# Placing the matmul operands, opening stages with two output tiles at once, and re-queuing the mixers' products in a four-part transformer kernel

## The chip, the cores and the metric

The kernel runs on one core of one Trainium2 chip. The metric is the device time of one execution in microseconds (us). Engines: PE (TensorE) multiplies matrices, DVE (VectorE) and ACT (ScalarE) work element by element, POOL (GpSimd) does some additions, and SP issues most of the DMAs.

## The reference

One block with four mixers over 512 tokens of 1024 features, and then two hybrid layers. All dense products are fp32. Cut to what matters:

```python
def first_block(x, p, ...):
    z = rms_norm(x, norm1_g) @ w_in
    mix = concat([gmlp(z), rglru(z), hgrn2(z), pool(z)])
    x = x + mix @ w_out
    hf = causal_dwconv(rms_norm(x, norm2_g) @ w_up)
    x = x + (gelu(gate half) * value half) @ w_down
    x = x + (p @ w_pe) * sigmoid(rms_norm(x, norm3_g) @ w_pg)
    return rms_norm(x, final_g)

def hybrid_layer(x, ...):                       # twice
    proj = (_rms(x) * norm1_g) @ w_in           # attention, rwkv, retention, gates
    mixed = g[0] * (attention(...) @ w_attn_o) \
          + g[1] * (rwkv7_time_mix(...) @ w_rwkv_o) \
          + g[2] * (retention(...) @ w_ret_o)   # g = sigmoid(gates)
    x = x + mixed @ w_out
    h2 = _rms(x) * norm2_g
    return x + (silu(h2 @ w_ffn_gate) * (h2 @ w_ffn_up)) @ w_ffn_down
```

## The kernel before, in words

Activations lie with features on the 128 partitions and the 512 tokens along the free axis, so a 1024-feature array is eight tiles `x0` to `x7`. Each fp32 operand is written as a sum of two numbers in a shorter format (`hi` and `lo`), and a product is three matmuls: hi by hi (L135), hi by lo (L136), lo by hi (L137), in `mac`. A dense output tile over 1024 features is thus 24 matmuls of 128x128 weights and 128x512 moving data; the down products run over 22 hidden tiles, 66 matmuls.

Weights arrive from DRAM in chunks of 128x1024 (`fetch`, L114, three buffers `wraw`). `chunk` splits each into `whi` (a cast on ACT, L125) and `wlo` (a subtraction on DVE, L126), with two buffers each. Accumulators are four PSUM banks `mm` and four `ps`. The moving operands are the split tiles `x#h/x#l` (pool `xgp`), the hidden tiles `h#h/h#l` (pools `f1h`, `f2h`), the attention and retention outputs `o` (pool `op`), the mixed tiles `mx#h/mx#l` (pool `mp`) and the rwkv outputs, which reuse the `BK` tiles (pool `rk`).

The place of a tile in a partition follows from the sizes of the pools opened ahead of it. In bytes, counted from a multiple of 256: the weight buffers and all `x` tiles begin at 32; `h`, `o` and `mx` at 160; `BK` at 64.

The order of work on an engine is set by a planner at compile time: it goes through the instructions by their place in the program, takes the earliest that by its own estimate of durations is ready, and passes over those that are not; each engine then runs its list in that order and waits where an operand is not there yet. `high_priority(offset=300)` moves a weight chunk's load and conversion 300 places forward. On top of this the program itself holds a queue of fill tasks (`queue`, `pump`, `flush`): in each hybrid layer 24 gate tiles (`gate_tile`) and 16 projections of the attention and retention stage, put out a few microseconds' worth at a time between the steps of the rwkv, attention and retention mixers, each task with a stated cost.

The norm of a stage is applied after its product: `acc_sq` (L219 ACT square, L220 addition on POOL) sums the squares of eight tiles, `norm_scale` sums over features with small matmuls (L210), takes a reciprocal root in a dozen small DVE steps and broadcasts it (L195) as `rb`, by which the first outputs of the stage are scaled. In the program `norm_scale` stands ahead of the stage's first product. Stages that begin so: `ffn1` (w_up), its gate product (w_pg), each layer's projections (`rwkv`, from the scales at the end of `ffn1` or `ffn2`), `ffn2`.

In a layer, `rwkv` comes first (with `rwkv_inverse`, which keeps DVE busy with small steps and eight long transposes, L952 and L956), then `out_b` (w_rwkv_o), `branches` (attention projections, `attention`, `retention`, `combine`, w_out) and `ffn2`. `retention` works through four chunks of 128 tokens; in each, the normalised output `ot` (`head_rms`, L662 to L671) is transposed on PE (L1366), multiplied by the gate (L1370) and split (L1371, L1372). `combine` (L1378 on) then runs both remaining output products, w_attn_o and w_ret_o, and adds gates and the stored rwkv part.

Of the kernel before, what the change touches and what calls it, by code (L numbers as in the profile page):

```python
# [10 lines left out]
F32 = mybir.dt.float32  # L11
# [9 lines left out]
P = 128  # L21
# [13 lines left out]
class Kern:  # L35
# [38 lines left out]

    def tap(self, name, ap):
        if name in self.taps:
            self.nc.sync.dma_start(self.taps[name], ap)
# [33 lines left out]
    def fetch(self, src):  # L111
        raw = self.tile(self.wp, [P, 1024], "wraw", bufs=3)
# [4 lines left out]
    def chunk(self, src):  # L117
# [4 lines left out]
        hi = self.tile(self.wp, [P, 1024], "whi", F32R)  # L122
        lo = self.tile(self.wp, [P, 1024], "wlo", F32R)
# [15 lines left out]
    def dense(self, wname, m, xs, kcuts=None):  # L139
# [9 lines left out]
        return ps  # L149

# [62 lines left out]
    def acc_sq(self, acc, x, i, eng=None):  # L213
# [45 lines left out]
    def mixers1(self, c2, x, xg, rb, pe):  # L259
# [4 lines left out]
        self.tb = c2.enter_context(tc.tile_pool(name="b1tt", bufs=12))  # L264
# [408 lines left out]
    def ffn1(self, x, acc, xg, pe, xs_p):  # L673
        tc, nc, io, V = self.tc, self.nc, self.io, self.vec
        rb = self.norm_scale(acc)
        with tc.tile_pool(name="f1h", bufs=1) as hp, tc.tile_pool(name="f1t", bufs=2) as fp:
            hid = []
            for j in range(FT):
                r = []
                for half in range(2):  # L680
                    m = half * FT + j
                    ps = self.dense("w_up", 2 * j + half, xg)
# [13 lines left out]
            for m in range(DT):  # L696
# [3 lines left out]
                self.acc_sq(acc, x[m], m)  # L700
        rb = self.norm_scale(acc)

        a3 = self.tile(self.xp, [P, T], "acc", bufs=2)
        a4 = self.tile(xs_p, [P, T], "acc4")
        xd = self.tile(self.dr, [DT, P, T], "xres", bufs=4)
        with tc.tile_pool(name="f1g", bufs=2) as gp:
            for m in range(DT):
                ps = self.dense("w_pg", m, xg)
# [12 lines left out]


# [10 lines left out]
            r4b = self.tile(gp, [P, T], "r4b", bufs=1)  # L733
# [3 lines left out]
        return xd, out, rb  # L737


    def layer(self, l, xd, xg, rb, out=None):  # L740
        tc, nc, io = self.tc, self.nc, self.io
        self.l, self.xgs, self.rb = l, xg, rb
        self.gates = self.tile(self.dr, [24, P, T], "gates", bufs=2)
        self.mixb = self.tile(self.dr, [DT, P, T], "mixb", bufs=2)
        with ExitStack() as c:
            self.rwkv(c)
# [18 lines left out]
    def rwkv(self, c):  # L765
        tc, nc, io, V, l = self.tc, self.nc, self.io, self.V2, self.l
        kp = c.enter_context(tc.tile_pool(name="rk", bufs=1))
        for g in range(24):
            g = (g + 8) % 24
            self.queue(5.2, lambda g=g: self.gate_tile(g))  # L770
        self.tb = c.enter_context(tc.tile_pool(name="rt", bufs=12))
# [25 lines left out]
        AR = self.tile(kp, [P, 4, NCH, P], "AR")  # L797
        BK = [self.tile(kp, [P, NCH, P], f"BK{p}") for p in range(4)]
# [5 lines left out]
        def shifted(m, mu):  # L804
            ps = self.proj(m)
# [8 lines left out]
        wd_t = shifted(18, 12)  # L814
# [3 lines left out]
        gd_t = shifted(19, 13)  # L818
# [294 lines left out]

    def evac(self, dst, ps, scale=1.0):
# [7 lines left out]
    def branches(self, c, xd):  # L1122
        tc, nc, io, l = self.tc, self.nc, self.io, self.l
        op = c.enter_context(tc.tile_pool(name="op", bufs=1))
        with ExitStack() as c2:
            ap = c2.enter_context(tc.tile_pool(name="ap", bufs=1))
            rp = c2.enter_context(tc.tile_pool(name="rp", bufs=1))
            at = c2.enter_context(tc.tile_pool(name="at", bufs=4))
# [448 lines left out]
```

## Time and profile before

| | |
|---|---|
| median of three runs | 2609.47 us (2606.51 to 2609.70) |
| the profiled execution | 2611.01 us |
| its span, first to last instruction | 2609.2 us |
| PE busy | 2533.5 us, 97% |
| DVE, ACT, POOL busy | 1468.6, 912.1, 378.1 us |
| mean granted clock of PE | 0.992 |

The span is the time between the first and the last instruction of the profiled execution. A matmul's end is modelled in this profile, and consecutive matmuls overlap in it, so the pace of a stream of matmuls is read from the distances of their starts and not from their durations.

### The profile page before, as it was taken

The page shows a single profiled execution, that of the slowest core. Times are in us where ns is not written, and L with a number is a line of the kernel's source. Part 1 is how long each engine was busy: PE and PEld are TensorE (multiplying, and loading weights), DVE is VectorE, ACT ScalarE, POOL GpSimd, SP SyncE. Part 2 cuts the span into 40 slices and gives each one's busy share as a digit, 9 for nine tenths or more (in the row PEclk, how much of TensorE's full clock was granted, in tenths as well). Part 3 has the DMA queues.
Part 4 walks back from the last instruction along what each step waited for, and adds up shares of the span by engine and source line. Part 5 has one row for each costly group of instructions (what it writes and reads, how often), then busy time and mean ns, then how long its engine had stood idle before and what let it go on. Part 6 is the DMA issues. An engine that isn't in the chain of part 4 may idle for free. (4 is left out here: it accounts for less than half of the span.)

```text
span 2609.2 us, 33284 instructions
## 1 busy us (share of the span) xinstructions
PE 2533.5 (97%) x13104; PEld 2019.5 (77%) x13104; DVE 1468.6 (56%) x2512; ACT 912.1 (35%) x1370; POOL 378.1 (14%) x277
## 2 busy tenths in 40 slices
PE   8989999999999999999999999999999999999999
PEld 6777888887777777677788887777777677788887
DVE  8776666326787556565544433787556565444422
ACT  4343444325433334423322222433334423322211
POOL 2122111003110001005311101110001004211100
PEclk9999999999999999999999999999999999999999
DMA  4132332334224153235433234224153226332242
GB/s 151 60 110 85 96 97 96 95 98 145 93 77 134 56 180 97 73 100 192 129 97 97 95 122 132 82 82 134 58 178 93 73 95 201 128 97 97 95 121 91
DMA packets 99501, 282.51 MB, mean 108 GB/s; under 512 B 13200, under 2 KB 14224, under 8 KB 99216
## 3 DMA queue, kind: packets, MB, share of 16 engines
q1 hardware_dynamic: 97616, 277.52, 33.1%
q10 hardware_dynamic: 1728, 2.87, 0.3%
q8 instruction: 103, 1.69, 0.3%
q14 instruction: 54, 0.44, 0.1%
HBM read 244.42 MB, written 31.72 MB: 106 GB/s over the span
## 5 line engine op out<-in xcount | busy, mean ns | idle before, releaser
L125 ACT CAST whi<-wraw 128x1024 fp32r<-128x1024 f32 (+1 forms) x400 | 414.2, 1036 | 1101.4 <-PE mm L136 704.7
L126 DVE TENSOR_TENSOR wlo<-wraw,whi 128x1024 fp32r<-128x1024 f32 (+1 forms) x400 | 494.7, 1237 | 243.8 <-ACT whi L125 231.8
L1410 POOL TENSOR_TENSOR fg<-fg,rb 128x512 f32<-128x512 f32 x44 | 78.3, 1779 | 396.1 <-ACT fg L1409 396.1
L220 POOL TENSOR_TENSOR acc<-acc,sq 128x512 f32<-128x512 f32 x49 | 78.4, 1601 | 325.8 <-ACT sq L219 325.8
L135 PE MATMUL mm<-x0h,whi 128*128 128x512 f32 x286 | 117.7, 412 | 8.1 <-ACT x0h L165 8.1
L137 PE MATMUL mm<-x0h,wlo 128*128 128x512 f32 x286 | 115.1, 403 | 5.5 <-DVE wlo L126 5.4
L136 PE MATMUL mm<-x0l,whi 128*128 128x512 f32 x286 | 113.3, 396 | 1.3 <-DVE x0l L169 1.3
L136 PE MATMUL mm<-x5l,whi 128*128 128x512 f32 x286 | 112.9, 395 | 1.6 <-DVE x5l L169 1.6
L136 PE MATMUL mm<-x1l,whi 128*128 128x512 f32 x286 | 113.8, 398 | 0.3 <-DVE x1l L169 0.3
L1412 DVE TENSOR_TENSOR fg<-fg,mm 128x512 f32<-128x512 f32 x44 | 30.3, 688 | 148.9 <-PE mm L137 148.9
L136 PE MATMUL mm<-x2l,whi 128*128 128x512 f32 x286 | 113.9, 398 | 0.0
L135 PE MATMUL mm<-x1h,whi 128*128 128x512 f32 x286 | 113.8, 398 | 0.0
L135 PE MATMUL mm<-x7h,whi 128*128 128x512 f32 x286 | 113.6, 397 | 0.0
L136 PE MATMUL mm<-x3l,whi 128*128 128x512 f32 x286 | 112.8, 394 | 0.7 <-DVE x3l L169 0.7
L137 PE MATMUL mm<-x1h,wlo 128*128 128x512 f32 x286 | 113.4, 396 | 0.0
L137 PE MATMUL mm<-x2h,wlo 128*128 128x512 f32 x286 | 113.3, 396 | 0.0
L135 PE MATMUL mm<-x3h,whi 128*128 128x512 f32 x286 | 112.9, 395 | 0.0
L135 PE MATMUL mm<-x2h,whi 128*128 128x512 f32 x286 | 112.8, 394 | 0.0
L137 PE MATMUL mm<-x6h,wlo 128*128 128x512 f32 x286 | 112.8, 394 | 0.0
L136 PE MATMUL mm<-x7l,whi 128*128 128x512 f32 x286 | 112.7, 394 | 0.0
L137 PE MATMUL mm<-x5h,wlo 128*128 128x512 f32 x286 | 112.7, 394 | 0.0
L136 PE MATMUL mm<-x6l,whi 128*128 128x512 f32 x286 | 112.7, 394 | 0.0
(758 smaller groups left out, 6057.0 us busy)
## 6 DMA issues: line engine op xcount, KB each, us to landing
wraw<-in_w_in_dram SPq DMA_DIRECT2D x138, 512.0 KB, 3.5
wraw<-in_w_ffn_dram SPq DMA_DIRECT2D x88, 512.0 KB, 3.5
wraw<-in_w_up_dram SPq DMA_DIRECT2D x44, 512.0 KB, 3.4
wraw<-in_w_ffn_down_dram SPq DMA_DIRECT2D x32, 448.0 KB, 3.4
wraw<-in_w_out_dram SPq DMA_DIRECT2D x24, 512.0 KB, 3.6
gates<-gt SPq DMA_DIRECT2D x48, 256.0 KB, 2.2
gt<-xres SPq DMA_DIRECT2D x32, 256.0 KB, 3.4
cg<-gates SPq DMA_DIRECT2D x32, 256.0 KB, 2.9
```

What stands on the lines that cost most here:

```text
L125: nc.scalar.copy(hi[:, :n], raw[:, :n])
L126: nc.vector.tensor_tensor(lo[:, :n], raw[:, :n], hi[:, :n].bitcast(F32), ALU.subtract)
L135: self.nc.tensor.matmul(ps, hi[:, c], xh, start=first and k == 0, stop=False)
L136: self.nc.tensor.matmul(ps, hi[:, c], xl, start=False, stop=False)
L137: self.nc.tensor.matmul(ps, lo[:, c], xh, start=False, stop=last and k == n - 1)
L220: (eng or nc.gpsimd).tensor_tensor(acc, acc, s, ALU.add)
L1410: nc.gpsimd.tensor_tensor(g, g, rb, ALU.mult)
L1412: nc.vector.tensor_tensor(g, g, ps, ALU.mult)
```

## The change

Tiles are moved by small pads (128 bytes before the hidden tiles and the pool `op`, 224 bytes before `BK`), which puts `h`, `o`, `mx` and `BK` at 32 from a multiple of 256. The chunk pipeline has two `wraw` buffers and three each of `whi` and `wlo`, one buffer more in all; the room comes from shorter rings of temporaries (`b1tt` 12 to 11, `rt` 12 to 10, the attention and retention rings 4 and 5 to one of 7). `opening` runs the first two output tiles of a stage over all input tiles but the last, then both over the last; it is used in `ffn1` (twice), `rwkv`, ahead of w_out and in `ffn2`, and it stands ahead of `norm_scale` in the program. The scales of a layer's projections are worked out at their first use. The last addition of the squares is on DVE instead of POOL. Half of the attention's output product (`out_a`, four of eight tiles) is two fill tasks of the queue, with the sum stored to DRAM (`mixa`). The retention's transposes run one chunk later (`turn`), with one pump per chunk instead of two, and the queue is flushed ahead of the last. Gates 0 to 7 are queued ahead of 16 to 23, and the first attention block pumps 2 us more after each softmax.

```diff
+    def pad(self, pool, n):
+        self.tile(pool, [P, n], "pad")
     def fetch(self, src):
-        raw = self.tile(self.wp, [P, 1024], "wraw", bufs=3)
+        raw = self.tile(self.wp, [P, 1024], "wraw", bufs=2)
...
-        hi = self.tile(self.wp, [P, 1024], "whi", F32R)
-        lo = self.tile(self.wp, [P, 1024], "wlo", F32R)
+        hi = self.tile(self.wp, [P, 1024], "whi", F32R, bufs=3)
+        lo = self.tile(self.wp, [P, 1024], "wlo", F32R, bufs=3)
...
+    def opening(self, calls, xs):
+        nc = self.nc
+        n = (len(xs) - 1) * P
+        last = self.tile(self.xp, [P, 2, 2, P], "rb", F32R, bufs=2)
+        ws = []
+        for i, (wname, m) in enumerate(calls):
+            raw = self.early.popleft() if self.early else self.fetch(self.io[wname][m])
+            hi = self.tile(self.wp, [P, 1024], "whi", F32R, bufs=3)
+            lo = self.tile(self.wp, [P, 1024], "wlo", F32R, bufs=3)
+            with self.tc.high_priority(offset=300):
+                for h, l, r in ((hi[:, :n], lo[:, :n], raw[:, :n]), (last[:, i, 0], last[:, i, 1], raw[:, n:])):
+                    nc.scalar.copy(h, r)
+                    nc.vector.tensor_tensor(l, r, h.bitcast(F32), ALU.subtract)
+            ps = self.tile(self.mm, [P, 512], "mm")
+            self.mac(ps, (hi, lo), xs[:-1], True, False)
+            ws.append(ps)
+        for i, ps in enumerate(ws):
+            self.mac(ps, (last[:, i, 0], last[:, i, 1]), xs[-1:], False, True)
+        return ws
...
-            (eng or nc.gpsimd).tensor_tensor(acc, acc, s, ALU.add)
+            (nc.vector if i == DT - 1 else eng or nc.gpsimd).tensor_tensor(acc, acc, s, ALU.add)
...
     def ffn1(self, x, acc, xg, pe, xs_p):
+        first = self.opening([("w_up", 0), ("w_up", 1)], xg)
         rb = self.norm_scale(acc)
...
+            self.pad(hp, 32)
...
-                    ps = self.dense("w_up", 2 * j + half, xg)
+                    ps = first[half] if j == 0 else self.dense("w_up", 2 * j + half, xg)
...
     def rwkv(self, c):
-            g = (g + 8) % 24
+            g = g + 8 if g < 8 else g - 8 if g < 16 else g
             self.queue(5.2, lambda g=g: self.gate_tile(g))
-        self.tb = c.enter_context(tc.tile_pool(name="rt", bufs=12))
+        self.tb = c.enter_context(tc.tile_pool(name="rt", bufs=10))
...
+        self.pad(kp, 56)
         BK = [self.tile(kp, [P, NCH, P], f"BK{p}") for p in range(4)]
...
+        first = self.opening([(f"w_in_2{l}", 18), (f"w_in_2{l}", 19)], self.xgs)
+        wd_t = shifted(18, 12, first[0])
...
+    def out_a(self, oa):
+        nc, io, l = self.nc, self.io, self.l
+        def tiles(j):
+            w = self.chunk(io[f"w_attn_o_2{l}"][j])
+            for i in range(2):
+                m = 2 * j + i
+                o = slice(i * 512, (i + 1) * 512)
+                g, b = (self.tile(self.xp, [P, T], t, bufs=2) for t in ("gt", "sq"))
+                nc.sync.dma_start(g, self.gates[m])
+                nc.sync.dma_start(b, self.mixb[m])
+                ps = self.tile(self.mm, [P, 512], "mm")
+                self.mac(ps, (w[0][:, o], w[1][:, o]), oa, True, True)
+                nc.vector.scalar_tensor_tensor(g, g, 1.0, ps, ALU.add, ALU.mult)
+                nc.gpsimd.tensor_tensor(b, b, g, ALU.add)
+                nc.sync.dma_start(self.mixa[m], b)
+        for j in range(DT // 4):
+            self.queue(5.6, lambda j=j: tiles(j))
...
-                self.pump(self.pa)
+                self.pump(self.pa if b else self.pa + 2.0)
...
     def retention(self, rp, op, q, k, vt, sg, cn):
+        def turn(w, ot):
...
-            self.pump(self.pr)
             ot = self.tmp(self.tb)
             self.head_rms(ot...)
-            pt = self.psum()
-            for p in range(4):
-                nc.tensor.transpose(pt[:, p * P:(p + 1) * P], ot[:, p * P:(p + 1) * P], self.ident)
             self.pump(self.pr)
...
+            if w:
+                turn(w - 1, last)
+            last = ot
+        self.flush()
+        turn(NW - 1, last)
...
     def combine(self, oa, oc, mp):
-            ca = self.chunk(io[f"w_attn_o_2{l}"][j])
-            cc = self.chunk(io[f"w_ret_o_2{l}"][j])
+            ready = j < DT // 4
+            ws = [(self.chunk(io[f"w_ret_o_2{l}"][j]), oc, 16)]
+            if not ready:
+                ws.append((self.chunk(io[f"w_attn_o_2{l}"][j]), oa, 0))
...
+                nc.sync.dma_start(b, self.mixa[m] if ready else self.mixb[m])
...
     def ffn2(self, xd, acc, xg, out):
+        first = self.opening([(f"w_ffn_2{l}", 0), (f"w_ffn_2{l}", 1)], xg)
         rb = self.norm_scale(acc)
...
-        return xd2, xg, self.norm_scale(acc)
+        return xd2, xg, lambda: self.norm_scale(acc)
```

## Rows read from the trace of the kernel before

**Rows 1.** The page: span, and busy time by engine.
```profile
span 2609.2 us, 33284 instructions
...
PE 2533.5 (97%) x13104; PEld 2019.5 (77%) x13104; DVE 1468.6 (56%) x2512; ACT 912.1 (35%) x1370; POOL 378.1 (14%) x277
```
**Rows 2.** Timeline, start and duration: two first matmuls 24 apart, on `x` tiles.
```profile
310.71 0.39 PE L135 MATMUL mm<-x0h,whi 128*128 128x512 f32 x1
...
316.15 0.39 PE L135 MATMUL mm<-x0h,whi 128*128 128x512 f32 x1
```
**Rows 3.** Timeline: two first matmuls 66 apart, on hidden tiles (w_down).
```profile
514.66 0.40 PE L135 MATMUL mm<-h0h,whi 128*128 128x512 f32 x1
...
530.06 0.40 PE L135 MATMUL mm<-h0h,whi 128*128 128x512 f32 x1
```
**Rows 4.** Timeline: two first matmuls 24 apart, on the mixed tiles (w_out).
```profile
2204.62 0.40 PE L135 MATMUL mm<-mx0h,whi 128*128 128x512 f32 x1
...
2210.22 0.40 PE L135 MATMUL mm<-mx0h,whi 128*128 128x512 f32 x1
```
**Rows 5.** Waits of PE: who for whom, us in total, times, longest.
```profile
PE ps L210 <- POOL acc L220: 7.3, 6, 2.6
PE mm L137 <- DVE wlo L126: 6.6, 7, 2.2
PE ps L1248 <- ACT as L1239: 6.6, 4, 2.8
PE ps L1366 <- DVE t L671: 6.2, 8, 1.5
...
PE mm L135 <- ACT o L1371: 2.9, 2, 1.4
...
PE ps L837 <- ACT wd L816: 1.7, 1, 1.7
```
**Rows 6.** Groups of PE: count, busy us and mean ns; idle before.
```profile
L137 PE MATMUL mm<-o,wlo 128*128 128x512 f32 x128 | 51.6, 403 | 1.3 <-DVE wlo L126 1.2
...
L137 PE MATMUL mm<-BK,wlo 128*128 128x512 f32 x64 | 25.3, 395 | 0.0
...
L137 PE MATMUL mm<-h0h,wlo 128*128 128x512 f32 x24 | 9.6, 398 | 0.0
...
L136 PE MATMUL mm<-mx7l,whi 128*128 128x512 f32 x16 | 6.6, 410 | 0.0
```
**Rows 7.** Timeline where `ffn1` begins; in brackets the idle time before.
```profile
226.63 2.05 POOL L220 TENSOR_TENSOR acc<-acc,sq 128x512 f32<-128x512 f32 x1 [4.67 <-ACT sq L219]
227.48 1.75 DVE L169 SCALAR_TENSOR_TENSOR x7l<-x,pv,x7h 128x512 fp32r<-128x512 f32 x1
...
228.74 1.05 PE L210 MATMUL ps<-ones,acc 128*128 128x1 f32 x8 [2.60 <-POOL acc L220]
```
**Rows 8.** Stretches: us, busy and count of PE, PEld, DVE, ACT, POOL; clock; DMA.
```profile
230.00:233.50 3.50, 3.50 (x10) 2.73 (x9) 1.81 (x11) 0.00 (x0) 0.00 (x0) 0.51 0.09 30
...
2243.90:2247.30 3.40, 3.40 (x10) 2.53 (x9) 1.60 (x10) 0.00 (x0) 0.00 (x0) 0.50 0.10 35
```
**Rows 9.** Timeline of PE where the first layer begins.
```profile
637.66 0.39 PE L135 MATMUL mm<-x0h,whi 128*128 128x512 f32 x1
...
649.87 1.05 PE L210 MATMUL ps<-ones,acc 128*128 128x1 f32 x8 [0.58 <-POOL acc L220]
```
**Rows 10.** Timeline of DVE at the end of the first layer's `rwkv_inverse`.
```profile
811.25 4.01 DVE L952 STREAM_TRANSPOSE SC<-iQ 32x1024 f32<-32x1024 f32 x2
...
815.90 1.22 DVE L126 TENSOR_TENSOR wlo<-wraw,whi 128x1024 fp32r<-128x1024 f32 x1
```
**Rows 11.** The page: the two conversions of a weight chunk, and the loads.
```profile
L125 ACT CAST whi<-wraw 128x1024 fp32r<-128x1024 f32 (+1 forms) x400 | 414.2, 1036 | 1101.4 <-PE mm L136 704.7
L126 DVE TENSOR_TENSOR wlo<-wraw,whi 128x1024 fp32r<-128x1024 f32 (+1 forms) x400 | 494.7, 1237 | 243.8 <-ACT whi L125 231.8
...
wraw<-in_w_in_dram SPq DMA_DIRECT2D x138, 512.0 KB, 3.5
```

More of the change, by code (lines that the diff above doesn't have):

```diff
@@ L149, in dense, with rb @@
         return ps
+    def opening(self, calls, xs):
[17 more added lines that the diff above has]
+        return ws
+    @property
+    def rb(self):
+        if callable(self.rb_):
+            self.rb_ = self.rb_()
+        return self.rb_
     def dense2(self, wname, xs, use):
@@ L700, in ffn1 @@
                 self.acc_sq(acc, x[m], m)
+        first = self.opening([("w_pg", 0), ("w_pg", 1)], xg)
         rb = self.norm_scale(acc)
         a3 = self.tile(self.xp, [P, T], "acc", bufs=2)
-        a4 = self.tile(xs_p, [P, T], "acc4")
+        a4 = self.tile(self.xp, [P, T], "acc", bufs=2)
         xd = self.tile(self.dr, [DT, P, T], "xres", bufs=4)
@@ L736, in ffn1 @@
             nc.sync.dma_start(self.r4d, r4b)
-        return xd, out, rb
+            return rb
+        return xd, out, scales
     def layer(self, l, xd, xg, rb, out=None):
         tc, nc, io = self.tc, self.nc, self.io
-        self.l, self.xgs, self.rb = l, xg, rb
+        self.l, self.xgs, self.rb_ = l, xg, rb
         self.gates = self.tile(self.dr, [24, P, T], "gates", bufs=2)
         self.mixb = self.tile(self.dr, [DT, P, T], "mixb", bufs=2)
+        self.mixa = self.tile(self.dr, [DT // 2, P, T], "mixa", bufs=2)
         with ExitStack() as c:
@@ L817, in rwkv @@
         nc.scalar.copy(wd[64:P], wd_t[64:P])
-        gd_t = shifted(19, 13)
+        gd_t = shifted(19, 13, first[1])
         gd = self.tile(kp, [P, T], "gd")
@@ L1135, in branches @@
             self.tb = rt
+            self.out_a(oa)
             oc = self.retention(rp, op, *r)
-            self.flush()
         mp = c.enter_context(tc.tile_pool(name="mp", bufs=1, reuse_waits="tile"))
@@ L1145, in branches @@
             nc.sync.dma_start(r4, self.r4d)
+        first = self.opening([(f"w_out_2{l}", 0), (f"w_out_2{l}", 1)], mix)
         for m in range(DT):
-            ps = self.dense(f"w_out_2{l}", m, mix)
+            ps = first[m] if m < 2 else self.dense(f"w_out_2{l}", m, mix)
             x = self.tile(self.xp, [P, T], "gt", bufs=2)
@@ L1318, in retention @@
         ol = self.tile(op, [P, 4, T], "o3", F32R)
-        R = None
+        def turn(w, ot):
+            c = slice(w * P, (w + 1) * P)
+            pt = self.psum()
+            for p in range(4):
+                nc.tensor.transpose(pt[:, p * P:(p + 1) * P], ot[:, p * P:(p + 1) * P], self.ident)
+            y = self.tmp(self.tb)
+            y3 = y.rearrange("p (g t) -> p g t", g=4)
+            nc.vector.tensor_tensor(y3, pt.rearrange("p (g t) -> p g t", g=4), sg[:, :, c], ALU.mult)
+            nc.scalar.copy(oh[:, :, c], y3)
+            nc.vector.tensor_tensor(ol[:, :, c], y3, oh[:, :, c].bitcast(F32), ALU.subtract)
+        R, last = None, None
         for w in range(NW):
@@ L1386, in combine @@
                 o = slice(i * 512, (i + 1) * 512)
-                g = []
-                for n, src in enumerate((self.gates[m], self.gates[16 + m], self.mixb[m])):
-                    t = self.tile(mp, [P, T], f"cg{n}", bufs=2)
-                    nc.sync.dma_start(t, src)
-                    g.append(t)
-                for n, (w, x) in enumerate(((ca, oa), (cc, oc))):
+                b = self.tile(mp, [P, T], "cg", bufs=2)
+                nc.sync.dma_start(b, self.mixa[m] if ready else self.mixb[m])
+                for w, x, n in ws:
+                    g = self.tile(mp, [P, T], f"cg{n}", bufs=2)
+                    nc.sync.dma_start(g, self.gates[n + m])
                     ps = self.tile(self.mm, [P, 512], "mm")
                     self.mac(ps, (w[0][:, o], w[1][:, o]), x, True, True)
-                    nc.vector.scalar_tensor_tensor(g[n], g[n], 1.0, ps, ALU.add, ALU.mult)
-                    nc.gpsimd.tensor_tensor(g[2], g[2], g[n], ALU.add)
-                mix.append(self.split(mp, g[2], f"mx{m}", 0.5))
+                    nc.vector.scalar_tensor_tensor(g, g, 1.0, ps, ALU.add, ALU.mult)
+                    nc.gpsimd.tensor_tensor(b, b, g, ALU.add)
+                mix.append(self.split(mp, b, f"mx{m}", 0.5))
         return mix
```

26 lines of the change are left out of this document (11 added, 15 removed).

## The prediction

> **What bounds the kernel now.** I read the page first: PE is busy in 2533.5 of 2609.2 us, the other engines in at most 56% [rows 1]. So there are only two ways to gain: matmuls that follow each other faster, or gaps of PE that close. Most of the kernel is an unbroken stream of 128x512 matmuls; the pace of that stream is read from starts in the timeline. On `x` tiles 24 matmuls take 316.15 - 310.71 = 5.44 us, 226.7 ns each [rows 2]. On hidden tiles 66 take 15.40 us, 233.3 ns each [rows 3], and on mixed tiles 24 take 5.60 us, also 233.3 ns [rows 4]. The instruction, shape, weights' buffers and clock are the same; what differs in the program is the place of the moving tile, 32 or 160 bytes past a multiple of 256. Then the view of waits: of about 76 us in which PE is not busy, the rows that this change can touch hold 7.3 + 6.6 + 6.6 + 6.2 + 2.9 + 1.7 = 31.3 us [rows 5]. Last the view of stretches: behind seven of the stalls that the change touches there is a stretch of 3.3 to 3.5 us in which the granted clock is 0.50 to 0.51, the 1.2 GHz level, after PE had stood idle (first and last of the seven in [rows 8]). At half pace such a stretch does half its work: 3.4 x 0.5 = 1.7 us lost each.
>
> **Part by part.** The sum is made against the profiled execution, 2611.0 us, which lies 1.5 us over the median of the runs.
>
> *Aligned tiles.* The pads put `h`, `o`, `mx` and `BK` where `x` already is, 32 past a multiple of 256. Counts: 24 matmuls on each of 66 operands of hidden tiles (22 tiles, three forms) make 1584; 16 on each of 24 forms of mixed tiles 384; three forms of `o` with 128 each 384; three of `BK` with 64 each 192 [rows 6]. That is 2544 matmuls. Gaining 233.3 - 226.7 = 6.6 ns each gives 16.8 us; `o` runs partly between other work, so I take **16.5 us**. Bounds: nothing if place is not the cause, 16.8 if it is; no row shows a pace over 233.3, so I exclude a loss. Counted in 512 bytes the hidden tiles will stand 256 from where the `x` tiles stand, a place that no row shows; I take the full gain since `x` tiles stand at every multiple of 512 relative to their weights and all run at 226.7 ns, but keep the lower end for the range.
>
> Against this stands a statement of the Trainium skill, "SBUF — State Buffer", section Specifications (TRN2): the memory is read in lines of 16 bytes, and crossing lines is what costs. By that both places start on a line, and the term would be 0. The rows show two paces for one instruction, so the page does not explain this trace; it counts as the first rival.
>
> *Opened stages.* At `ffn1` POOL's last addition of squares takes 2.05 us and PE waits 2.60 us for it, since the norm's small matmuls stand ahead of the rest of the first product [rows 7]. With `opening` 42 matmuls of two output tiles, 9.5 us, stand ahead of them, on tiles `x0` to `x6`; `x7l`, which here takes 1.75 us because it runs beside POOL, is then ready. The six such waits hold 7.3 us and the wait for `wd` at the first layer's start 1.7 us [rows 5]: all of it goes, 9.0 us. Four of the half-clock stretches stand behind these (in `ffn1`, in the first layer's start, in the second layer's start, in the last `ffn2`): 4 x 1.7 = 6.8 us. At the first layer's start PE also starves for `x` tiles: between 637.66 and 649.87 there are 28 matmuls, 6.3 us of work in 12.2, so 5.9 us are lost [rows 9]. Two tiles opened together have six matmuls for each arriving `x` tile instead of three, but the tiles still come from the same ACT and DVE steps; I take 4 of 5.9, with 2 and 5.9 as ends. Sum **19.8 us**. What it adds, one small cast and one small subtraction for each of 16 chunks (eight openings of two), lies beside the matmuls, 5.44 us a chunk against 1.04 us on ACT and 1.24 on DVE [rows 2, 11]. Without that cover it would cost 16 x 0.3 = 5 us, an estimate from an eighth of a whole conversion (0.13 and 0.15 us). Ahead of w_out PE has no such wait among the rows, so the opening there is worth 0. Late next is `rb`: four accumulators hold four tiles, 21.8 us of work, before PE must wait for it.
>
> *Three converted buffers.* At the end of `rwkv_inverse` two transposes hold DVE for 4.01 us and the conversion queued behind them comes at 815.90, too late [rows 10]; such waits sum to 6.6 us [rows 5], and two of the half-clock stretches follow them, 3.4 us. A third buffer lets a conversion stand one chunk, 5.44 us, earlier, more than the 4.01 us. I take **8.5 of 10.0 us**; ends 4 and 10. The price is a load less in flight: a `wraw` buffer comes free after its subtraction, and 3.5 + 1.04 + 1.24 = 5.8 us later its next content is converted [rows 11]; two buffers must do this once in two chunks, 10.9 us. So it is covered with 5.1 us to spare.
>
> *Retention one chunk later.* PE waits 6.2 us for `ot` ahead of the eight groups of transposes [rows 5]. With a chunk in between these go, and for the last chunk the flush does it: one pump per chunk puts out 16 us of credit, so two gates and both `out_a` tasks, some 21 us, remain for it. I take **5.5 us**; ends 3 and 6.2. What is late next is the split of the last chunk: the 2.9 us in front of the first w_ret_o matmul [rows 5] and the half-clock stretch behind it stay, since `out_a` now stands ahead of the transposes and not behind them.
>
> *Half of the attention's product in the queue.* The matmuls are the same 96 per layer, now used as fill. Added are four stores of 256 KB per layer on SP's queue and, on DVE and POOL, the same steps as before in `combine`. SP's loads queue behind `out_a`'s reads of gates and of the rwkv part, which were stored long before; I cost it at **0**, hidden by matmuls, between a loss of 4 us (eight stores, half a microsecond of issue each) and a gain of 2.9 us. The gate order only serves this, 0.
>
> *More fill in the first attention block.* The wait for the softmax, 6.6 us in four places [rows 5], gets 2 x 2 us more fill per layer, but from a queue that must then do without it later. I take **1.5 us**; ends 0 and 6.6.
>
> *Shorter rings.* In the order of the kernel before at most 10 of the 12 `rt` buffers are live at a time (counted from first to last use in the program's order), so 10 do; of `b1tt` all 12 are live in a seventh of that stage, so one less will delay something there. No row shows it. I take a loss of **4 us** with 0 and 12 as ends.
>
> Sum: 16.5 + 19.8 + 8.5 + 5.5 + 1.5 - 4 = 47.8 us. 2611.0 - 47.8 = 2563.2 for the profiled execution, 1.5 less against the median: **2562 us**.
>
> **Rivals.** *Place is not the cause* (0.14). Then 16.5 us are missing: 2578. For it: tiles at 256 past the others in 512 are untried, and the page above. Against: two paces that go with place in every stage.
>
> *The gaps come back elsewhere* (0.19). The planner works from its own durations and was wrong at each stall; a new order can be wrong at other places, as with POOL's 2.05 us. If half of the 33.8 us of gaps returns: 2579. For it: DVE is busy 56% on average and more in the mixers, and the pieces share DVE. Against: `opening` gives 9.5 us of work against waits of at most 2.6. If `opening` changes nothing in the planned order, 19.8 us fail and the time is 2582; I count it here.
>
> *Two `wraw` buffers are too few* (0.03), slower. It decides from the point where a load needs over 10.9 - 2.3 = 8.6 us to land instead of 3.5 [rows 11]. At 10 us, each pair of chunks would take 12.3 instead of 10.9 us; over the 400 chunks 200 x 1.4 = 280 us less the 47.8 of gain. Already with a fifth of the chunks so late the loss is 56 us, and the time 2618. Against: no wait of PE for a load stands among the rows.
>
> *A wash* (0.02), within 0.2% (5 us, about what a measurement of this kernel can tell from no change): place fails, most gaps return and the rings cost 12.
>
> **How the numbers follow.** The forecast has 0.62: 2562, of itself from 2548 (all upper ends: 5.9, 10, 6.2, 6.6 and no ring loss add some 15 us) to 2574. The rivals reach to 2582, and a mix of the first two to 2595. The range from 2546 to 2588 leaves out about 2 in 10. Faster 0.95, same 0.02, slower 0.03.
>
> **What would show it.** Right: 66 matmuls on hidden tiles in 14.96 us; no wait of L210 for the squares; no wait of L137 for `wlo` beside the transposes; fewer stretches at 0.50; L1366 without waits. Wrong: hidden tiles still at 233 ns; a new row in PE's waits over 3 us, above all for `x` tiles at the layers' start, for `whi` by loads, or for temporaries in the first stage.

## The result, and the profile after

| | before | after |
|---|---|---|
| median of the runs | 2609.59 us (2606.51 to 2612.95, 4 runs) | 2569.11 us (2564.61 to 2569.77, 4 runs) |
| ratio after to before | | 0.9842, 95% interval 0.9826 to 0.9858 |
| profiled execution, its span | | 2564.61 us, 2562.8 us |

The change is faster by 40.5 us. The forecast was 2562 us, from 2546 to 2588. On a second chip the kernel after took 2565.99 us (2562.18 to 2571.5, 4 runs) against 2611.96, ratio 0.9824 (0.9804 to 0.9845). The profiled execution of the kernel after is the fastest of its four.

The page of the kernel after, against [rows 1]: PE is busy 31.5 us less, of a span that is 46.4 us shorter.

```profile
span 2562.8 us, 33418 instructions
...
PE 2502.0 (98%) x13104; PEld 2022.7 (79%) x13104; DVE 1487.7 (58%) x2535; ACT 912.8 (36%) x1386; POOL 356.2 (14%) x270
```

**Pace.** Two stretches of 100 us, inside the first and the last of the three stages on hidden tiles, in the kernel after. The columns are the stretch, its length, busy time and count of PE, PEld, DVE, ACT and POOL, then the granted clock and the DMA. Read the count of PE: 443. At the 233.3 ns of [rows 3] it would be about 430. Between starts the mean is 226.7 ns in each stage, the pace of [rows 2].

```profile
470.00:570.00 100.00, 100.00 (x443) 82.84 (x442) 31.70 (x34) 28.02 (x34) 7.78 (x5) 1.00 0.34 97
...
2445.00:2545.00 100.00, 100.00 (x443) 82.81 (x442) 27.66 (x28) 20.38 (x21) 0.00 (x0) 1.00 0.41 123
```

**Waits.** What PE waits for in the kernel after (us in total, times, longest), against [rows 5]. The additions of squares, `wd`, the softmax's `as` and the retention's `ot` ahead of its transposes are gone from the list. `wlo` went from 6.6 to 3.5, and 2.9 of those 3.5 stand in another place, in `combine` (2.21 and 0.71 us). New or larger: `o` (L1394, L1395), the retention's own matmuls behind `head_rms` (L1413, L1421), and `whi`. The wait for `ad` at L1359 only looks new: it stands at the transposes of the retention's values, where the kernel before waits 2.9 us (last line, a view of the kernel before).

```profile
...
PE mm L139 <- ACT o L1394: 3.8, 2, 2.2
PE mm L141 <- DVE wlo L130: 3.5, 4, 2.2
PE ps L1413 <- DVE t L706: 3.4, 4, 0.8
PE ps L1421 <- DVE t L706: 2.4, 2, 1.2
PE ps L1359 <- DVE ad L1303: 2.4, 2, 1.2
...
PE mm L140 <- DVE x4l L203: 1.8, 1, 1.8
PE mm L139 <- ACT whi L129: 1.7, 2, 1.3
...
PE mm L140 <- DVE o L1395: 1.6, 2, 0.8
```

```profile
PE ps L1292 <- DVE t L1118: 2.9, 2, 1.9
```

**An opened stage.** The timeline where `ffn1` begins, against [rows 7]: the last addition is on DVE and takes 0.68 us, `x7l` beside no POOL work takes 0.74 instead of 1.75, and PE comes to the norm's matmuls at 235.06 with no idle time ahead of them (a bracket would say so).

```profile
228.12 0.68 DVE L255 TENSOR_TENSOR acc<-acc,sq 128x512 f32<-128x512 f32 x1
228.72 0.74 DVE L203 SCALAR_TENSOR_TENSOR x7l<-x,pv,x7h 128x512 fp32r<-128x512 f32 x1
...
235.06 0.94 PE L244 MATMUL ps<-ones,acc 128*128 128x1 f32 x8
```

**The end of the first layer's `rwkv_inverse`**, DVE's timeline, against [rows 10]: the transposes still hold DVE, 4.06 and 2.08 us, but a conversion now stands at 804.90, ahead of them, and the next at 812.80. PE waits at most 0.5 us there.

```profile
804.90 1.22 DVE L130 TENSOR_TENSOR wlo<-wraw,whi 128x1024 fp32r<-128x1024 f32 x1
806.14 4.06 DVE L997 STREAM_TRANSPOSE SC<-iQ 32x1024 f32<-32x1024 f32 x2
...
812.80 1.20 DVE L130 TENSOR_TENSOR wlo<-wraw,whi 128x1024 fp32r<-128x1024 f32 x1
```

**What is left at half clock.** Stretches of the kernel after, columns as above. Of the nine in the kernel before, two lie in its first stage and are still there. Of the other seven, of which [rows 8] has the first and the last, two are left: the one at the first layer's start has moved ahead, from behind the wait for `wd` to behind waits for `x` tiles (first line), and the one at the first layer's retention's end stays (second). The other two lines are new places: the retention's end in the second layer, twice as long as the others, and `combine`. Where such stretches fall differs between executions: a second profile of the same kernel (run 5 below) has the one at the first layer's retention's end twice as long, none at the second's, and two more in the second layer, at 1784 and 2006 us.

```profile
633.60:636.90 3.30, 3.04 (x8) 2.23 (x8) 3.30 (x5) 2.06 (x3) 1.62 (x1) 0.50 0.34 129
1155.80:1159.20 3.40, 3.34 (x8) 2.67 (x9) 0.70 (x3) 0.00 (x0) 0.66 (x1) 0.50 0.90 261
2115.00:2121.70 6.70, 5.96 (x14) 4.46 (x14) 1.62 (x3) 0.00 (x0) 1.28 (x1) 0.50 0.92 306
2145.70:2149.00 3.30, 3.30 (x9) 2.54 (x9) 1.47 (x3) 0.63 (x1) 1.99 (x1) 0.50 0.83 287
```

PE's timeline ahead of the third line: after the last chunk's transposes PE has nothing but matmuls that need their output.

```profile
2111.41 0.60 PE L1390 MATMUL ps<-ident,t 128*128 128x128 f32 x4
2114.21 1.05 PE L139 MATMUL mm<-o,whi 128*128 128x512 f32 x3 [2.20 <-ACT o L1394]
2115.99 0.80 PE L140 MATMUL mm<-o,whi 128*128 128x512 f32 x1 [0.74 <-DVE o L1395]
```

### The profile page after: what moved, and what is told of

The parts are those of the page before. It is cut to its first block, busy times and chain, and to the rows that moved or that the text cites. A ratio compares the mean times of both kernels' runs of the same rounds, so it can differ in the third digit from the quotient of the medians.

```text
span 2562.8 us, 33418 instructions
## 1 busy us (share of the span) xinstructions
PE 2502.0 (98%) x13104; PEld 2022.7 (79%) x13104; DVE 1487.7 (58%) x2535; ACT 912.8 (36%) x1386; POOL 356.2 (14%) x270
## 4 chain that ended last, share of the span: by engine, by line
PE 78%; DVE 12%; issue 3%; ACT 3%; DMA 1%; POOL 0%; SPq 0%; DVEq 0%; ACTq 0%; POOLq 0%
PE mm L139 23%; PE mm L141 23%; PE mm L140 23%; DVE wlo L130 3%; ACT whi L129 1%; DVE iQ L993 1%; DVE iT L991 1%; PE ps L1320 1%; PE ps L1107 1%; PE ps L1067 1%; PE ps L1095 1%; PE ps L1416 1%; PE ps L944 0%; PE ps L582 0%; DVE t L855 0%
## 5 line engine op out<-in xcount | busy, mean ns | idle before, releaser
L129 ACT CAST whi<-wraw 128x1024 fp32r<-128x1024 f32 (+1 forms) x384 | 397.8, 1036 | 1003.2 <-PE mm L140 864.3
L130 DVE TENSOR_TENSOR wlo<-wraw,whi 128x1024 fp32r<-128x1024 f32 (+1 forms) x384 | 469.8, 1224 | 234.2 <-ACT whi L129 225.9
L1487 POOL TENSOR_TENSOR fg<-fg,rb 128x512 f32<-128x512 f32 x44 | 77.8, 1769 | 401.4 <-ACT fg L1486 401.4
L140 PE MATMUL mm<-x4l,whi 128*128 128x512 f32 x286 | 111.5, 390 | 1.8 <-DVE x4l L203 1.8
L141 PE MATMUL mm<-x3h,wlo 128*128 128x512 f32 x286 | 112.7, 394 | 0.0
L139 PE MATMUL mm<-x4h,whi 128*128 128x512 f32 x286 | 112.4, 393 | 0.0
L139 PE MATMUL mm<-x5h,whi 128*128 128x512 f32 x286 | 112.0, 392 | 0.0
L139 PE MATMUL mm<-x6h,whi 128*128 128x512 f32 x286 | 112.0, 392 | 0.0
```

Source lines behind the costliest of these rows:

```text
L129: nc.scalar.copy(hi[:, :n], raw[:, :n])
L130: nc.vector.tensor_tensor(lo[:, :n], raw[:, :n], hi[:, :n].bitcast(F32), ALU.subtract)
L139: self.nc.tensor.matmul(ps, hi[:, c], xh, start=first and k == 0, stop=False)
L140: self.nc.tensor.matmul(ps, hi[:, c], xl, start=False, stop=False)
L141: self.nc.tensor.matmul(ps, lo[:, c], xh, start=False, stop=last and k == n - 1)
L1487: nc.gpsimd.tensor_tensor(g, g, rb, ALU.mult)
```

## The experiments

The theory at the outset: the forecast's terms hold, part by part, and the tail of the retention is what the new order left open. The rivals: one part carries all of it, or a part costs what another gives. So parts were undone one at a time in the kernel after, the pads were put alone into the kernel before, and the order at the retention's end was varied. Each timed kernel was run four or five times; kernels 2 and 3, made for their pace, ran once. A ratio is to the runs of the kernel before on its own chip, with a 95% interval.

### 1. The pads alone

```
 f1h, f2h, op:   + self.pad(hp or op, 32)
 rk, ahead of BK: + self.pad(kp, 56)
```

> The kernel before, with the four pads alone (hidden tiles, o and mixed tiles, BK at 32 past a multiple of 256 as the x tiles are); everything else stays. Theory (the place of the moving tile sets the pace): 2544 matmuls gain 6.6 ns each, 66 matmuls on hidden tiles take 14.96 us instead of 15.40, and the time falls by 16.5 us, from 2609.5 to 2593 (2591 to 2595). Rival 1 (place is not the cause, the new order is): 2609.5, pace still 233.3 ns. Rival 2 (the pace comes, but the faster stream waits more for DVE and ACT at its end): pace 226.7 ns and a time of 2597 to 2604.

Measured: 2600.69 us against 2612.65, ratio 0.9951 (0.9938 to 0.9965), 12.0 us less. The pace came in full: each of the three stages on hidden tiles is 3.5 us shorter, and 66 matmuls take 14.96 us. The time is that of rival 2, but not for its reason: PE comes to the same stalls earlier and waits in them as before (7.4 us for `acc`, 6.4 for `ot`, 7.0 for `as`). Part of the 4.5 us that are missing is in the clock. In the profiled execution the stretches at half clock sum to 57 us, against 43 in the profile before; one of the new ones:

```profile
1025.30:1028.60 3.30, 3.18 (x9) 2.57 (x10) 1.34 (x2) 3.30 (x8) 0.00 (x0) 0.50 0.35 80
```

14 us more at half pace lose up to 7 us. But that execution has the lowest mean granted clock among the five, 0.989; the one with the highest, 0.992, took 2595.41 us, 17.2 less than the kernel before. Over all five the mean is 0.9904 against 0.9912 in the nine runs before, by estimate 2 of the 4.5 us; the rest stays open.

### 2 and 3. Which place counts

```
 kernel 2: f1h pad 32 -> 48; f2h 32 -> 16 (first layer), 36 (second); op 32 -> 8, 33
 kernel 3: + self.pad(self.cst, 8) ahead of everything; f2h 32 -> 24, 40
```

> The kernel after, with other pads: hidden tiles of ffn1 at 96, of ffn2 at 224 (first layer) and 64 (second), o and mixed tiles at 192 (first) and 64 (second) past a multiple of 256; weights and x tiles stay at 32. Theory (only the weights' own place modulo 256 is fast): all of these run at 232 to 233.3 ns, and the time rises by 2352 x 6.6 ns = 15.5 us, to about 2584. Rival 1 (several places are fast, 160 was merely a bad one): one or more of the five stages stays at 226.7 ns, and the rise is less by 3.5 us for each of the three hidden stages. Rival 2 (the pace worsens with the distance): different paces between 227 and 240 ns.

> The kernel after, with 32 bytes ahead of everything: weights, x tiles, BK, o, mixed tiles and the hidden tiles of ffn1 all stand at 64 past a multiple of 256; the pad of ffn2's hidden tiles is chosen so that they stand at 32 in the first layer and at 96 in the second. Theory R (what counts is that moving tile and weights have the same place modulo 256): everything stays at 226.7 ns but the two ffn2 down stages, which go to about 233 ns: 1056 x 6.6 ns = 7 us more, about 2576. Rival A (what counts is the moving tile's own place, 32): x tiles, BK, o, mixed tiles and ffn1's hidden tiles go to 233 ns, only the first ffn2's hidden tiles stay at 226.7 ns: some 9000 matmuls x 6.6 ns = 60 us more, about 2629.

Kernel 2, a single execution: 2580.15 us. Stages on hidden tiles, columns as above: 439, 431 and 430 matmuls in 100 us.

```profile
475.00:575.00 100.00, 100.00 (x439) 82.04 (x438) 32.30 (x35) 28.41 (x35) 9.49 (x6) 1.00 0.33 98
1490.00:1590.00 100.00, 100.00 (x431) 80.12 (x430) 29.77 (x32) 26.31 (x32) 7.68 (x5) 1.00 0.42 128
2455.00:2555.00 100.00, 100.00 (x430) 80.34 (x429) 25.80 (x25) 19.52 (x20) 0.00 (x0) 1.00 0.41 127
```

From start to start: 228.9 ns at 96, 233.3 at 224, 233.3 at 64; `o` and mixed tiles 234.3 at 192 and 233.3 at 64. Kernel 3, a single execution: 2573.77 us, and the same stages:

```profile
475.00:575.00 100.00, 100.00 (x443) 82.81 (x442) 32.31 (x35) 28.39 (x35) 9.29 (x6) 1.00 0.34 100
1490.00:1590.00 100.00, 100.00 (x430) 80.55 (x429) 32.29 (x35) 27.59 (x35) 8.46 (x6) 1.00 0.41 127
2455.00:2555.00 100.00, 100.00 (x430) 80.34 (x429) 27.45 (x27) 19.49 (x20) 0.00 (x0) 1.00 0.40 123
```

With the weights at 64, hidden tiles at 64 are fast (226.7), and those at 32, the fast place of the kernel after, are slow (233.3). Theory R holds, rival A falls: what counts is the distance between moving tile and weights, modulo 256. Of the expectations for kernel 2 none holds whole: only the weights' own place is fully fast, but there are levels between, and the pace does not simply worsen with the distance. Measured distances: 0 gives 226.7 ns; 64 gives 228.9; 32, 128, 192 and 224 give 233.3 (128 is that of [rows 3, 4]); 160 gives 234.3.

### 4. The last queued piece behind the last transposes

```
-        self.flush()
+        self.flush(len(self.fill) - 1)
         turn(NW - 1, last)
+        self.flush()
```

> The kernel after, with one step moved: in the flush at the end of the retention the last queued task (two output tiles of the attention's product, 24 matmuls, 5.4 us) is put behind the last chunk's transposes instead of ahead of them. Theory (the order is the cause of PE's idle time there): the waits for o after the last transposes, 1.9 to 2.2 us and 0.7 to 1.2 us in each layer, and the half-clock stretch behind them are covered by the 5.4 us: 4 to 5 us less in each layer, 2560 to 2562 against 2569. Rival 1 (DVE is the bound there: the moved task's weight conversion and its gate step delay the split): the waits move to the first w_ret_o chunk or into the combine, 0 to 3 us less, 2566 to 2569. Rival 2 (PE now waits for head_rms ahead of the last transposes, as it did in the kernel before): no gain or 1 to 3 us lost.

Measured: 2561.23 us against 2612.65, ratio 0.9805 (0.9791 to 0.9818). The time is the theory's, and the stretches at half clock at the retention's end are gone. Against the two ratios of the kernel after this is 5 to 10 us less; the interval of the second, 0.9824, overlaps. But rival 2 is in it too: PE's waits now have the transposes waiting for `head_rms`, and the low half of `o` is still late.

```profile
PE ps L1390 <- DVE t L706: 2.6, 2, 1.3
...
PE mm L140 <- DVE o L1395: 2.3, 2, 1.2
```

### 5 to 8. Parts undone, on one chip

```
 6:  - first = self.opening(...)   in all five places; norm_scale and scales at once
 7:  wraw bufs 2 -> 3;  whi, wlo bufs 3 -> 2
 8:  + self.pump(self.pr) ahead of head_rms;  turn(w, ot) at once
```

> The kernel after, unchanged, as the base of the three runs that follow it on the same chip. Expected 2565 to 2570 us and a ratio of 0.983 to 0.986.

> The kernel after without its openings: each stage makes its norm first and then its first product, as in the kernel before; the last addition of squares stays on DVE. Theory (the openings close the waits for the squares, for wd and the half-clock stretches behind them): 12 to 20 us more than the kernel after, 2581 to 2589; L214 waits for acc again in six places. Rival 1 (the last addition on DVE instead of POOL, 2.05 us, already closes them): less than 5 us more, up to 2574, and no waits for acc. Rival 2 (openings gain at the stages' start, but the time is lost at the x tiles' splits): 5 to 12 us more.

> The kernel after with three wraw and two whi and two wlo buffers, as in the kernel before; rings stay at 10 and 11. Theory (the third converted buffer covers the two transposes that hold DVE at the end of rwkv_inverse): waits for wlo there come back, 5 to 10 us more than the kernel after, 2574 to 2579. Rival 1 (the new order of the work covers them anyway): within 3 us of the kernel after. Rival 2 (the smaller load reserve costs as much as the third buffer gives): 0 to 5 us less.

> The kernel after, with the retention's outputs transposed in their own chunk and a pump on either side of the transposes' preparation, as in the kernel before; the attention's half product stays in the queue. Theory (turning one chunk later removes the six waits for ot, 6.2 us, but the waits of the last chunk's split stay, and DVE's chain now delays scores and kz by 1.0 to 1.4 us in three chunks of each layer, 6.8 us): it is nearly a wash, within 4 us of the kernel after, 2565 to 2573. Rival 1 (turning later gains the 5.5 us that were forecast): 2574 to 2576. Rival 2 (with out_a as fill the old order is better, since nothing then stands behind the last split): 2560 to 2565.

The kernel after: 2565.99 us on this chip, ratio 0.9824, just under the expected range. **Without openings** 2576.51, ratio 0.9860 (0.9843 to 0.9878), 10.5 us more, and each of its four runs is slower than each of the four of the kernel after: rival 2's size, but not its reason. The one wait for `acc` (L244 in these kernels) is 1.0 us, so rival 1 is right that without openings the addition on DVE closes those; what came back is 2.5 us of waits for `mx7h` ahead of w_out and 1.4 us for the norm's `rsq` at the first layer's start.

**With the old chunk buffers** 2583.2, ratio 0.9892 (0.9876 to 0.9907), 17.2 us more. PE waits 9.6 us for `wlo` and 7.9 us for `whi`. Rows of its waits, then the first layer's inverse in its timeline, where the conversion is again queued behind the transposes:

```profile
PE mm L141 <- DVE wlo L130: 9.6, 7, 2.2
...
PE mm L139 <- ACT whi L129: 7.9, 3, 4.1
```

```profile
798.62 4.01 DVE L997 STREAM_TRANSPOSE SC<-iQ 32x1024 f32<-32x1024 f32 x2
...
803.27 1.22 DVE L130 TENSOR_TENSOR wlo<-wraw,whi 128x1024 fp32r<-128x1024 f32 x1
...
804.54 0.64 PE L141 MATMUL mm<-x0h,wlo 128*128 128x512 f32 x1 [2.15 <-DVE wlo L130]
...
1187.17 0.80 PE L139 MATMUL mm<-o,whi 128*128 128x512 f32 x1 [4.06 <-ACT whi L129]
```

The last line is in `combine`, where the kernel before waits for `whi` only once, 1.3 us: the third buffer also covers a stall that another part of the change makes. Theory right in kind, too small.

**Turned at once** 2576.48, ratio 0.9863 (0.9847 to 0.9880), 10.5 us more, half a microsecond over the highest of the three expectations. With two pumps a chunk the queue runs out before the last chunk, and its transposes wait 6.8 us in each layer:

```profile
PE ps L1390 <- DVE t L706: 20.1, 6, 6.8
```

### 9. Without the half product in the queue

```
-            self.out_a(oa)
-            ready = j < DT // 4
+            ready = False
```

> The kernel after without the attention's half product in the queue: all of it is computed in combine, as in the kernel before; everything else stays. The kernel after has 2566 to 2569 us. Theory (the half product is the fill that turning one chunk later needs at the retention's end, so the two parts hang together): the wait for the last chunk's head_rms comes back in full ahead of the last transposes, 4 to 8 us in each layer less what the combine gains, 6 to 14 us more, 2573 to 2582. Rival 1 (worth nothing, as forecast): 2565 to 2571. Rival 2 (its own steps on DVE and POOL are what delays the last splits): 3 to 8 us less, 2559 to 2565.

Measured: 2554.03 us (2552.08 to 2554.34, 4 runs) against 2611.0, ratio 0.9778 (0.9765 to 0.9792). That is beyond rival 2's range and **faster than both kernels**: the ratio is 0.0046 or 0.0064 below the two ratios of the kernel after, 12 or 17 us. Theory fell: the fill at the retention's end does not need the half product. Ahead of the last transposes stand gates instead, and between the last chunk's scores and these transposes PE is busy 20.4 of 21.3 us.

What the kernel after loses lies behind the transposes. The stretches from there to the first w_out matmul, first and second layer; of the kernel after:

```profile
1152.18:1192.74 40.56, 35.51 (x147) 28.10 (x146) 24.68 (x28) 9.52 (x14) 19.11 (x14) 0.96 0.80 259
2111.74:2154.97 43.23, 38.34 (x148) 30.03 (x146) 22.88 (x31) 11.01 (x17) 16.17 (x13) 0.88 0.73 237
```

and of this one:

```profile
1139.91:1186.43 46.52, 44.53 (x196) 36.02 (x194) 24.07 (x33) 11.88 (x17) 24.35 (x15) 1.00 0.72 231
2099.04:2144.57 45.53, 43.94 (x196) 36.17 (x194) 25.66 (x32) 12.26 (x18) 23.09 (x14) 1.00 0.73 236
```

The kernel after has 144 product matmuls there, 32.6 us at 226.7 ns, in 40.56 and 43.23 us: 7.9 and 10.6 us lost. Without the half product 192, 43.5 us, in 46.52 and 45.53: 3.0 and 2.0 us lost. The difference is 13.5 us, and about half of it is clock: granted 0.96 and 0.88 in the first two lines, 1.00 in the other two. A second profile of the kernel after (run 5) loses 10.5 and 10.1 us there. Outside these stretches this kernel loses 3.1 us more than the kernel after, so that the two profiled spans differ by 10.4 us.

Rival 2 has a part in it. At the first layer's retention's end in the kernel after, DVE's weight conversion at 1153.30 takes 1.90 us instead of 1.22, beside POOL's addition for the half product (1152.86 to 1154.13), and only behind it DVE splits the low half of `o`, for which PE waits 0.81 us. Without the half product PE waits there for the high half alone, 1.59 us in each layer.

How the rest is lost, in the timeline of the kernel after, in the second layer's `combine`. The columns: start, duration, engine, what it does, in brackets the idle time before and what ended it.

```profile
2137.98 6.14 SPq L1467 DMA_DIRECT2D cg<-gates  x4
...
2139.75 4.02 POOL L1471 TENSOR_TENSOR cg<-cg,cg 128x512 f32<-128x512 f32 x3 [3.57 <-DMA cg<-mixb]
...
2141.68 0.69 DVE L1470 SCALAR_TENSOR_TENSOR cg<-cg,mm 128x512 f32<-128x512 f32 x1 [2.29 <-DMA cg<-gates]
...
2142.45 0.63 ACT L199 ACTIVATE mx4h<-cg 128x512 fp32r<-128x512 f32 x1 [3.38 <-POOL cg L1471]
2142.99 1.03 ACT L129 CAST whi<-wraw 128x1024 fp32r<-128x1024 f32 x1
...
2143.12 1.21 DVE L203 SCALAR_TENSOR_TENSOR mx4l<-cg,mx4h 128x512 fp32r<-128x512 f32 x1 [0.75 <-ACT mx4h L199]
2144.25 1.21 DVE L130 TENSOR_TENSOR wlo<-wraw,whi 128x1024 fp32r<-128x1024 f32 x1
...
2144.07 0.50 PE L139 MATMUL mm<-o,whi 128*128 128x512 f32 x1 [1.26 <-ACT whi L129]
```

Read from below: PE waits for a weight chunk's `whi`, which needs nothing of the mix. But on ACT it stands behind the split of `mx4`, which waits for POOL's addition, which waits for loads of gates and of the rwkv part; DVE is held the same way. A tile whose attention product is already done has 12 matmuls, 2.7 us, to cover its loads (3.1 us for `cg` from the gates, 4.5 from the stored half), its gate step, its addition (1.3 us) and its split, with two buffers of each kind. A tile with both products has 5.4 us. That the loads start late is seen in SP's own waits in the second layer's stretch, first the kernel after, then the one without the half product: in both, loads of gates wait until POOL's addition gives a buffer back. Without the half product the waits are longer in sum, and the matmuls cover them.

```profile
SPq L1467 <- POOL cg L1471: 12.8, 6, 3.7
```

```profile
SPq L1466 <- POOL cg L1470: 21.6, 12, 4.0
```

Which of the loads, the two buffers and the addition sets this pace was not tried apart.

### 10. The opened stages wholly undone

```
 as 6, and:
-            (nc.vector if i == DT - 1 else eng or nc.gpsimd).tensor_tensor(acc, ...)
+            (eng or nc.gpsimd).tensor_tensor(acc, ...)
```

> The kernel after without its openings, as in the second run of the call before (2576.5 us, 10.5 us over the kernel after), and the last addition of squares is put back on POOL as well, so that the whole part is undone. Theory (the 19.8 us forecast for the part hold, and the addition on DVE alone already closes half of it): waits of about 1.2 us for acc in six places, with the half-clock stretches behind them, 5 to 9 us more than without openings, 2582 to 2586. Rival 1 (the addition is worth nothing; the term of 19.8 us was too large): 2575 to 2579. Rival 2 (the addition on DVE delays the splits, POOL is better): 2570 to 2574.

Measured: 2585.24 us against 2611.0, ratio 0.9899 (0.9885 to 0.9913), the theory's. Six waits are back, as many and as long as in [rows 5]:

```profile
PE ps L244 <- POOL acc L255: 7.3, 6, 2.5
```

Against the two ratios of the kernel after, the whole part is worth 15 to 20 us; by the ratios, taking out the openings costs 9.4 of the 19.6 us, counted from the chip of run 5, and then taking the addition from DVE 10.2 more. In the other order the shares may differ: no run has openings with the addition on POOL.

### 11 and 12. Another order in `combine`

```
-        for j in range(DT // 2):            # retention's product first
+        for j in (2, 0, 1, 3):              # attention's product first where not done
 12: and the flush of 4
```

> The kernel after with the combine's chunks in the order 2, 0, 1, 3 instead of 0 to 3, and with the attention's product ahead of the retention's within a tile. Theory (what PE lacks behind the last transposes is any work that does not need the retention's output): 12 matmuls of the attention's product, 2.7 us, stand ahead of the first that needs it, so the waits for o, 1.9 to 2.4 and 1.0 us in each layer, shrink to under 1 us, and the half-clock stretches behind them go: 4 to 9 us less, 2558 to 2563. Rival 1 (DVE is the bound: its two weight conversions at once delay the split further): within 2 us of the kernel after. Rival 2 (the two tiles whose attention product is done, 2.7 us of PE each against 2.7 us or more of DVE, are worse in the middle): 1 to 4 us more.

> The kernel after with both orders: the last queued piece of the attention's product behind the last transposes (2561.2 us alone, ratio 0.9805), and the combine in the order of the run before. Theory (enough work stands behind the last split): the wait of 1.3 us for o goes as well, 1 to 4 us less than with the piece behind alone, a ratio of 0.979 to 0.980, 2557 to 2560. Rival (what is left at that place is the wait of 1.3 us for head_rms ahead of the transposes, which neither order covers, and the conversions on DVE): ratio 0.9800 to 0.9815.

Measured: 2561.04 us, ratio 0.9808 (0.9795 to 0.9821), and 2561.64, ratio 0.9809 (0.9795 to 0.9822). The first is the theory's: 12 matmuls that need no `o` of the retention close the wait for its high half, and 4.5 and 4.7 us are lost behind the transposes instead of 7.9 and 10.6. Against the two ratios of the kernel after that is 4 to 9 us less, with the interval of 0.9824 overlapping again. Together they give nothing more, as the rival said: the wait for `head_rms` ahead of the transposes (1.3 us in each layer) is back, and both share PE's new waits of 1.8 us in each layer's `combine` for an accumulator that DVE's gate step still holds. All three orders (4, 11 and 12) stay 7 to 8 us behind the kernel without the half product.

## Why the prediction was right, and where its steps were not

The sum was right because errors cancelled, and that is luck: against 47.8 us the medians differ by 40.5, and the profiled executions by 46.4, the one after being the fastest of its four. By its parts:

- **Aligned tiles**, 16.5: the pace is as forecast in every stage, and runs 2 and 3 show that place is the cause, so the first rival falls. Alone it gave 12.0 (9 to 16 by the interval); part of the rest went into stretches at half clock, which the step did not count. The doubt about the place 256 past in 512 bytes was not needed: the hidden tiles run at full pace there.
- **Opened stages**, 19.8: 15 to 20 measured for the part as a whole. The six waits for the squares are gone as forecast. The step did not price the addition on DVE, which alone closes most of them: with the openings gone, putting it back on POOL costs 10.2 us. The openings would have covered it at `ffn1`, where PE comes to the norm's matmuls 6 us after the last square is added. At the first layer's start, where 4 of 5.9 us were booked, the step was wrong: PE still waits 1.44, 1.10 and 1.76 us for `x0h`, `x0l` and `x4l`, 4.3 us, where without openings it waits 4.6 (of these 1.4 for `rsq`), and the half-clock stretch, which was to go, is there with openings and not without (in run 6 the granted clock is 1.00 from 630 to 680 us). The opening ahead of w_out, booked at 0, closes waits that the new `combine` makes.
- **Three converted buffers**, 8.5 with ends 4 and 10: mis-sized. Undone it costs 17.2 (11.2 between the two profiled spans). The inverse's waits are as forecast; the buffer also covers `combine`, where without it PE waits 7.9 us for `whi` against 1.3 in the kernel before. Two `wraw` buffers were enough: no wait of PE is put down to a load.
- **Retention one chunk later**, 5.5: the 6.2 us of waits ahead of the transposes went, but 5.8 us came at L1413 and L1421, state and keys held up behind `head_rms` on DVE, which were not forecast; so the waits by themselves do not show a gain. Undone it costs 10.5, since the old two pumps now empty the queue before the last chunk; so it is no clean measure of the term. What was to be late next is late, at the place named, and larger: 3.8 + 1.6 us for `o` instead of 2.9, and 10.2 us at half clock in one profile, 6.8 in the other, where the kernel before has 3.4.
- **Half of the attention's product in the queue**, 0 between a loss of 4 and a gain of 2.9: **this step failed**. In the kernel after it costs 12 to 17 us. "The same steps as before" on DVE and POOL, "hidden by matmuls", compared the steps and not their cover: what moved out of `combine` was PE's work (48 matmuls in each layer, not the 96 that the step counts), and for four of the eight tiles what stayed there lost half of its cover. Its own gate step and addition also fall beside the last splits of the retention.
- **More fill in the first attention block**, 1.5: not tried alone. The 6.6 us for `as` are gone from the list and nothing of their size came in that block, so it was rather under-sized; how much the other parts have in it stays open.
- **Shorter rings**, a loss of 4: not tried alone. With a ring of 11, no openings and the addition on POOL, the first hidden stage begins at 467.94 us, against 468.47 in the kernel before. But PE was at half clock for 13.7 us ahead of it, against 20.5, which is worth 3.4 us; so a loss of about 3 us may hide there. The ring of 10 stays open too.

Gains of 12, 15 to 20, 17 and 10.5 us less a loss of 12 to 17 make 38 to 48, around the 40.5 to 46 measured; the parts lean on each other, so this is no proof. The rival that had the gaps come back elsewhere was right in kind: they came back in `combine`.

## What to carry to other kernels

When work of the critical engine is moved out of a stage, ask what it covered there: the stage keeps all its loads, gate steps and splits, and they need the cover. Keep one piece of work that depends on nothing recent for the place behind the last dependent step, and look at which engine's queue a weight conversion stands in, behind what. And undo the parts even of a change that gained: here one part cost about a third of what the change gained.

## What the runs showed of the hardware

- The pace of one and the same matmul depends on the distance between moving tile and weights modulo 256 bytes: 226.7 ns at 0, 228.9 at 64, 233.3 at 32, 128, 192 and 224, 234.3 at 160. Each level but 226.7 and 233.3 comes from a single execution (run 2). With weights, `x` tiles and the hidden tiles of `ffn1` all moved by 32 bytes the pace stays at 226.7 (run 3). The statement of the Trainium skill weighed in the prediction ("SBUF — State Buffer", section Specifications (TRN2)) does not explain these rows: every one of these places is a multiple of 16. Why there are several levels stays open.
- A conversion of a chunk on DVE, 1.22 us, took 2.28 us beside a step of POOL, and PE waited 2.21 us for it. The timeline of the first layer's `combine` in the kernel after:

```profile
1182.03 1.72 POOL L1218 TENSOR_TENSOR gt<-gt,r 128x512 f32<-128x512 f32 x1
...
1182.55 2.28 DVE L130 TENSOR_TENSOR wlo<-wraw,whi 128x1024 fp32r<-128x1024 f32 x1
...
1184.88 0.50 PE L141 MATMUL mm<-o,wlo 128*128 128x512 f32 x1 [2.21 <-DVE wlo L130]
```

 By the Trainium skill ("SBUF — State Buffer", section Terms) DVE and GpSimd arbitrate for one shared pair of ports and the loser blocks; these rows come near to that, 1.06 us longer beside 1.20 us of overlap. It depends on who began first: in the same trace 40 conversions that began ahead of POOL's step L1487 and overlap it by 0.6 us or more took 1.23 us at most, and POOL's step took 1.78 us or more, where POOL's two-operand steps of that size that overlap no work of DVE take 1.28 to 1.30.
- The time at half clock is not fixed by the waits. Two profiles of the kernel after, with nearly the same waits, have 37 and 44 us of it; so the 57 us with the pads alone against 43 before, one profile each, do not show that a faster stream spends more time there.
